# A hybrid decoder layer on one core: paired sums in the up projection, two interleaved blocks at the head of each down projection, six raw weight slots

## The chip, the cores and the metric

The kernel runs on one core of a Trainium2 chip. A core has a matrix engine (TensorE, PE in the profile, with its weight loads shown apart as PEld), a vector engine (VectorE, DVE), a scalar engine (ScalarE, ACT), GpSimd (POOL, idle here) and SyncE (SP), which issues every DMA of this kernel. Each engine works through its own list of instructions in order; semaphores make one wait for another. The metric is the device time of one launch in microseconds. The kernel before takes 2044.98 us as the median of three runs (2036.12 to 2045.6).

## What is computed

One decoder layer over 2064 positions (16 learned meta tokens and 2048 inputs), width 1024, in fp32:

```python
u = rmsnorm(h) ; p = u @ w_in                       # 1024 -> 1792
y = concat(pool(p_pool), conformer(p_bval, p_bgate), rglru(p_cgate, p_cx))
h = h + y @ w_out
u = rmsnorm(h)
h = h + square(relu(u @ w_up)) @ w_down             # 1024 -> 4096 -> 1024
out = rmsnorm(h)[:, 16:]
```

The three mixers are a windowed mean with a small group matmul, a gated depthwise convolution of 31 taps with a layer norm, and a gated linear recurrence with a convolution of 4 taps. Channels lie on the 128 partitions, positions along the free dimension.

## The kernel before, in words

**Precision.** fp32 operands are split in two: `hi` is the value rounded to the matmul's fp32r type (ScalarE, line 108) and `lo` the rest (VectorE, line 109). A product is three matmuls: hi·hi, hi·lo, lo·hi. Every weight is loaded, split and used again in each chunk of positions, so splitting weights is the largest piece of work on ScalarE and VectorE.

**Stages.** The positions form four chunks (c = 0 to 3) of 512. The list `items` is the order of the matrix work: W blocks (input projection), O blocks (output projection), and for each chunk four groups g of four U units followed by eight D blocks. In chunk 2 the eight O blocks of chunk 3 stand inside the last group of D blocks, after the first four of them. In chunk 3 the last group of D blocks is done in two halves of 256 positions.

**A U unit** (`up_unit`, from line 761) makes two of the 32 tiles of 128 up-projection rows for 512 positions with seven products in place of eight (a Strassen-Winograd scheme on 2 x 2 blocks). The position side has seven operands, named B11, B21, B22, T1, T2, T3, T4, each a pair of tiles that `gen_norm2` makes once for a chunk; the weight side has seven blocks of 128 x 512, four of them sums that `gen_sums` computes once, in chunk 0, and stores in DRAM (`sums`). A product is 12 matmuls of 256 columns into its own PSUM bank (`mm_block`, line 285). VectorE adds the products up (line 782, seven adds of 256 columns), ScalarE applies relu and two squares, and VectorE makes the low half of the square (line 799). The results are two tiles of `U`, the inputs of the D blocks.

**A D block** (`mm_tile`, line 275) is 24 matmuls of 512 columns: eight input tiles k = 0 to 7, three matmuls each. The last two, k = 6 and 7, come from the unit just before it. VectorE adds the result to `h` (line 803).

**Weights.** `Weights` runs ahead of the matrix work: `wr` holds raw weight halves of 128 x 512 (WR = 4 slots, filled by SyncE, line 139), `wh` holds split ones (WH = 5 slots). A U product takes one half, a W, O or D block two. A raw slot is free again when its split on VectorE is done; a split slot when the last matmul on it is done.

**What sets the order.** The code is written in the order of `items`; after each item `pump` emits as much of the side work (mixers, normalisation, sums) as a budget allows. A scheduler then places the instructions of each engine by priority, which is the order in the program unless the code raises it, as their inputs and buffers come free in its own estimate. After that the order on each engine is fixed. PSUM has eight banks: five for the main products (`pm`), three for side work (`pb`).

## Time and profile before

| | before |
|---|---|
| median of 3 runs | 2044.98 us (2036.12 to 2045.6) |
| profiled execution | 2042.66 us, of which span 2040.9 us |
| PE busy | 1950.3 us (96%) |
| DVE busy | 1587.7 us (78%) |
| ACT busy | 1119.3 us (55%) |
| mean granted clock of TensorE | 0.985 |

In a row of a view by groups stand the line, engine, operation, the names written and read (buffer numbers left out), shapes and count, then busy time, the mean of one in ns, and the idle time just before. In the view of waits a row reads "engine, what waits, what it waited for: us in total, times, longest". In a timeline row stand the start, the busy time, and in brackets the idle time before it and what ended that. In a row of windows stand the stretch, its length, the busy time and count on each engine, the granted clock, the DMA engines' share and the GB/s. A PE that is shown busy may still be slow, since its records overlap and their ends are modelled.

### The profile page before, as it was taken

The numbers are of one execution on the slowest core, as the hardware profiler recorded it, in microseconds if no ns is written. First come the engines' busy times: TensorE is split into PE (matmuls) and PEld (weight loads), VectorE is DVE, ScalarE is ACT, GpSimd is POOL, SyncE is SP. The second block draws the span as 40 slices with busy tenths as digits, with TensorE's granted clock in tenths as the row PEclk, the third lists the DMA queues.
The fourth block names the chain that finished last, engine by engine and source line by source line (L and its number), as shares of the span: only waits on it lengthen the run. The fifth ranks groups of instructions, "written<-read, shape, count | busy, mean of one in ns | idle before, by whom it ended". The sixth has DMA issues, their size and how long they took to land.

```text
span 2040.9 us, 31716 instructions
## 1 busy us (share of the span) xinstructions
PE 1950.3 (96%) x11220; PEld 1694.6 (83%) x11220; DVE 1587.7 (78%) x2749; ACT 1119.3 (55%) x1904; POOL 0.2 (0%) x4
## 2 busy tenths in 40 slices
PE   8999889899998989999999999999999999999997
PEld 7888688788876779788898778888979878889797
DVE  8987787898988899874776799986768487556477
ACT  6654453635685535664575553664657346345364
POOL 0000000000000000000000000000000000000000
PEclk9999999999998999999999999999999999999999
DMA  6324588737534435353444633444435425544354
GB/s 201 114 78 154 175 255 282 223 114 237 164 106 143 146 98 156 98 156 103 150 119 129 193 102 113 140 117 133 139 108 160 123 79 171 153 131 143 112 167 148
DMA packets 166958, 297.79 MB, mean 146 GB/s; under 512 B 18320, under 2 KB 24592, under 8 KB 166800
## 3 DMA queue, kind: packets, MB, share of 16 engines
q1 hardware_dynamic: 166800, 295.77, 47.7%
q8 instruction: 88, 1.44, 0.3%
q14 instruction: 70, 0.57, 0.1%
HBM read 268.43 MB, written 27.26 MB: 145 GB/s over the span
## 4 chain that ended last, share of the span: by engine, by line
PE 49%; DVE 17%; DMA 15%; ACT 13%; issue 6%; SPq 0%; DVEq 0%; ACTq 0%
PE pm L275 41%; PE pm L285 6%; DMA wr<-sums 6%; DVE wh L109 5%; ACT wh L108 4%; DMA wr<-d_w_down 2%; DMA xr<-d_xr 2%; ACT fr L798 2%; ACT U L797 2%; DVE H L109 1%; ACT fr L795 1%; DVE U L799 1%; DMA s<-d_w_up 1%; DVE fr L782 1%; DVE rs L320 1%
## 5 line engine op out<-in xcount | busy, mean ns | idle before, releaser
L275 PE MATMUL pm<-U,wh 128*128 128x512 f32 (+1 forms) x4272 | 987.7, 390 | 42.4 <-ACT U L797 17.4
L275 PEld LDWEIGHTS pm<-U,wh 128*128 128x128 f32 x4272 | 785.0, 191 | 229.6 <-ACT U L797 24.3
L108 ACT ACTIVATE wh<-wr 128x512 fp32r<-128x512 f32 x876 | 538.2, 627 | 739.5 <-PE pm L275 485.2
L109 DVE TENSOR_TENSOR wh<-wr,wh 128x512 fp32r<-128x512 f32 x876 | 595.3, 686 | 217.1 <-ACT wh L108 213.4
L285 PE MATMUL pm<-H,wh 128*128 128x256 f32 x5376 | 662.6, 284 | 22.0 <-DVE wh L109 9.4
L285 PEld LDWEIGHTS pm<-H,wh 128*128 128x128 f32 x5376 | 650.5, 190 | 35.2 <-DVE wh L109 14.6
L275 PE MATMUL pm<-H,wh 128*128 128x512 f32 (+1 forms) x1344 | 268.0, 357 | 9.3 <-ACT H L373 7.5
L275 PEld LDWEIGHTS pm<-H,wh 128*128 128x128 f32 x1344 | 224.4, 190 | 49.5 <-ACT H L373 7.5
L517 DVE SCALAR_TENSOR_TENSOR ca<-Pbv,vec,ca 128x512 f32<-128x512 f32 x180 | 127.4, 745 | 0.0
L803 DVE TENSOR_TENSOR h<-h,pm 128x512 f32<-128x512 f32 (+1 forms) x106 | 71.3, 673 | 66.7 <-PE pm L275 66.2
L782 DVE TENSOR_TENSOR fr<-pm,q 128x256 f32<-128x256 f32 x256 | 106.5, 417 | 2.3 <-PE pm L285 1.3
L799 DVE TENSOR_TENSOR U<-fr,U 128x512 fp32r<-128x512 f32 x128 | 86.0, 687 | 23.1 <-ACT fr L798 21.7
L782 DVE TENSOR_TENSOR q<-pm,q 128x256 f32<-128x256 f32 x192 | 79.9, 416 | 7.3 <-ACT q L785 3.2
L797 ACT ACTIVATE U<-fr 128x512 fp32r<-128x512 f32 x128 | 77.1, 619 | 0.8
L798 ACT ACTIVATE fr<-fr 128x512 f32<-128x512 f32 x128 | 76.8, 617 | 0.2
L329 DVE TENSOR_TENSOR ss<-ss,fr 128x512 f32<-128x512 f32 (+1 forms) x84 | 53.9, 642 | 13.1 <-ACT fr L328 12.8
L320 DVE RECIPROCAL rs<-rs 128x512 f32<-128x512 f32 (+2 forms) x17 | 53.9, 3168 | 10.9 <-ACT rs L318 10.9
L793 ACT ACTIVATE fr<-fr 128x512 f32<-128x512 f32 x64 | 39.9, 624 | 7.3 <-DVE fr L782 6.7
L517 DVE SCALAR_TENSOR_TENSOR ca<-h,vec,ca 128x512 f32<-128x512 f32 x60 | 42.4, 745 | 0.0
L795 ACT ACTIVATE fr<-fr 128x512 f32<-128x512 f32 x64 | 39.6, 619 | 0.5
L328 ACT ACTIVATE fr<-h 128x512 f32<-128x512 f32 (+1 forms) x45 | 27.4, 617 | 15.8 <-DVE h L697 8.8
L551 DVE SCALAR_TENSOR_TENSOR t<-Pcx,vec,t 128x512 f32<-128x512 f32 x36 | 26.8, 744 | 0.4 <-ACT t L549 0.3
(199 smaller groups left out, 1003.3 us busy)
## 6 DMA issues: line engine op xcount, KB each, us to landing
wr<-d_w_down SPq DMA_DIRECT2D x272, 256.0 KB, 3.0
wr<-sums SPq DMA_DIRECT2D x256, 256.0 KB, 3.3
wr<-d_w_up SPq DMA_DIRECT2D x192, 256.0 KB, 3.2
wr<-d_w_in SPq DMA_DIRECT2D x92, 256.0 KB, 3.2
xr<-d_xr SPq DMA_DIRECT2D x56, 256.0 KB, 3.2
t<-d_w_up SPq DMA_DIRECT2D x32, 256.0 KB, 4.1
wr<-wo_fold SPq DMA_DIRECT2D x32, 256.0 KB, 2.8
wr<-d_w_out SPq DMA_DIRECT2D x32, 256.0 KB, 2.7
```

Source lines behind the costliest of these rows:

```text
L108: A.activation(out=hi, in_=src, func=AF.Copy)
L109: V.tensor_tensor(out=lo, in0=src, in1=hi.bitcast(F32), op=ALU.subtract)
L275: T.matmul(ps[:, : s1 - s0], w[k // 4][:, a, (k % 4) * P : (k % 4 + 1) * P], rhs[k][:, b, s0:s1], start=(k == 0 and j == 0), stop=(k == KB ...
L285: T.matmul(ps, w[:, a, k * P : (k + 1) * P], op[k // 2][:, b, (k % 2) * 256 : (k % 2) * 256 + 256], start=(k == 0 and j == 0), stop=(k == ...
L320: V.reciprocal(rs[:, c0:c1], rs[:, c0:c1])
L517: V.scalar_tensor_tensor(out=a, in0=o.ub[i][:, k : k + NT], scalar=vc("cw", i * CONVK + k), in1=a, op0=ALU.mult, op1=ALU.add)
L782: V.tensor_tensor(out=out, in0=ps, in1=x, op=ALU.add)
L795: A.activation(out=ra, in_=ra, func=AF.Relu)
L797: A.activation(out=f[:, 0], in_=r, func=AF.Square)
L798: A.activation(out=r, in_=r, func=AF.Square)
L799: V.tensor_tensor(out=f[:, 1], in0=r, in1=f[:, 0].bitcast(F32), op=ALU.subtract)
L803: V.tensor_tensor(out=h, in0=h, in1=ps[:, : s1 - s0], op=ALU.add)
```

## The change

- **Unit.** The products come in the order B11, B21, T2, T1, T3, B22, T4, the weight blocks with them. B21 and T2 share a PSUM bank and are added to the first product by one add of 512 columns; T1 and T3 likewise; T4 is put beside T1, across two neighbouring banks, and one add of 512 columns finishes the second output tile. So a unit has three adds of 512 columns and one of 256 in place of seven of 256. The first output tile is finished before the last product. A unit takes three of the four `fr` work tiles instead of two.
- **PSUM.** Four banks for `pm`, one tile of two banks for `pw` (a single buffer), two banks for `pb`.
- **Down projection.** The first two D blocks of a group run together (`mm_pair`): six k of the first, six k of the second, then k = 6, 7 of the first and of the second. In chunk 3's last group this holds for the first half only.
- **Weights.** WR is 6, WH is 4, and a weight split gets a priority 200 instructions higher. The run-ahead of loads (WH + WR) goes from 9 to 10.
- **Normalisation.** `gen_norm2` makes its operands in an order that suits the new order of products; the amounts of work are the same.
- **Chunk 2.** The O blocks of chunk 3 come after two D blocks instead of four.

```diff
-WR = 4
-WH = 5
+WR = 6
+WH = 4
 LA_SPLIT = WH
+EARLY = 200
 LA_DMA = WH + WR
...
-    pm = es.enter_context(tc.tile_pool(name="pm", bufs=5, space=bass.MemoryType.PSUM))
-    pb = es.enter_context(tc.tile_pool(name="pb", bufs=3, space=bass.MemoryType.PSUM))
+    pm = es.enter_context(tc.tile_pool(name="pm", bufs=4, space=bass.MemoryType.PSUM))
+    pw = es.enter_context(tc.tile_pool(name="pw", bufs=1, space=bass.MemoryType.PSUM))
+    pb = es.enter_context(tc.tile_pool(name="pb", bufs=2, space=bass.MemoryType.PSUM))
...
                 t = t_("wh", (2, 512), WH, F32R)
-                split(t[:, 0], t[:, 1], self.raw.pop(self.ns))
+                with tc.high_priority(EARLY):
+                    split(t[:, 0], t[:, 1], self.raw.pop(self.ns))
...
+    def mm_pair(ws, rhs, sub):
+        s0, s1 = sub
+        pss = [ps_main() for _ in ws]
+        for ks in (range(KB - 2), range(KB - 2, KB)):
+            for w, ps in zip(ws, pss):
+                for k in ks:
+                    for j, (a, b) in enumerate(PRODS):
+                        T.matmul(
+                            ps[:, : s1 - s0], w[k // 4][:, a, (k % 4) * P : (k % 4 + 1) * P], rhs[k][:, b, s0:s1],
+                            start=(k == 0 and j == 0), stop=(k == KB - 1 and j == 2),
+                        )
+        return pss
...
     def up_unit(o, u, h0):
...
-        p1, q, q7, s5 = (q_tile() for _ in range(4))
-        A.activation(out=p1, in_=product(), func=AF.Copy)
-        add(q, product(), p1)
-        add(q7, product(), q)
-        ps = product()
-        add(rb[:, rgt], ps, q7)
-        add(s5, ps, q)
-        add(ra[:, lft], product(), p1)
-        add(rb[:, lft], product(), q7)
-        A.activation(out=rb, in_=rb, func=AF.Relu)
-        add(ra[:, rgt], product(), s5)
-        A.activation(out=ra, in_=ra, func=AF.Relu)
-        for f, r in ((fb, rb), (fa, ra)):
+        def add2(out, ps, x):
+            V.tensor_tensor(
+                out=out.rearrange("p (a c) -> p a c", a=2), in0=ps.rearrange("p (a c) -> p a c", a=2),
+                in1=x.unsqueeze(1).broadcast_to([P, 2, 256]), op=ALU.add,
+            )
+        def square(f, r):
+            A.activation(out=r, in_=r, func=AF.Relu)
             A.activation(out=f[:, 0], in_=r, func=AF.Square)
             A.activation(out=r, in_=r, func=AF.Square)
             V.tensor_tensor(out=f[:, 1], in0=r, in1=f[:, 0].bitcast(F32), op=ALU.subtract)
+        px, py, pz = ps_main(), ps_main(), pw.tile([P, 1024], F32, name=nm("pw"), tag="pw")
+        product(px[:, :256])
+        A.activation(out=p1, in_=px[:, :256], func=AF.Copy)
+        product(py[:, :256])
+        product(py[:, 256:])
+        add2(ra, py, p1)
+        q = ra[:, 256:]
+        product(pz[:, 512:768])
+        product(pz[:, 768:])
+        add2(t2, pz[:, 512:], q)
+        px = ps_main()
+        product(px[:, :256])
+        V.tensor_tensor(out=q, in0=px[:, :256], in1=t2[:, :256], op=ALU.add)
+        square(fa, ra)
+        product(pz[:, 256:512])
+        add2(rb, pz[:, 256:768], t2[:, 256:])
+        square(fb, rb)
...
-                items.extend(down[:4])
+                items.extend(down[:2])
                 items.extend(("O", 3, j, full) for j in range(KB))
-                items.extend(down[4:])
+                items.extend(down[2:])
...
+        if kind == "D" and j % KB == 0 and s0 == 0:
+            wts.ahead(wi)
+            ws = [[wts.hl.pop(wi + 2 * i + q) for q in range(2)] for i in range(2)]
+            pss = mm_pair(ws, o.f, (s0, s1))
+            evac_d(o, j // KB, 0, pss[0], s0, s1)
+            held_ps.append(pss[1])
+            pump(BUD_D)
+            continue
```

How it moves instructions is shown at three places. In the names, `wh` is a split weight half and `wr` the raw one, `pm` and `pw` are PSUM tiles, `U` an input tile of the D blocks, `fr` a work tile of a unit, `H` a split operand of the U units, `s` and `t` work tiles of the normalisation. The numbers are the program's own and differ between the kernels.

First, PE where the second group of chunk 2 goes from its last U unit to its D blocks. Before (the unit's last product, then a whole D block, then the next):

```order
L285 MATMUL pm_2545_14066<-H_2162_11922,wh_2531_13983 128x256 x6
L275 MATMUL pm_2548_14092<-U_2428_13481,wh_2534_14002 128x512 x3
L275 MATMUL pm_2548_14092<-U_2429_13482,wh_2534_14002 128x512 x3
L275 MATMUL pm_2548_14092<-U_2459_13637,wh_2534_14002 128x512 x3
L275 MATMUL pm_2548_14092<-U_2460_13638,wh_2534_14002 128x512 x3
L275 MATMUL pm_2548_14092<-U_2488_13787,wh_2537_14022 128x512 x3
L275 MATMUL pm_2548_14092<-U_2489_13788,wh_2537_14022 128x512 x3
L275 MATMUL pm_2548_14092<-U_2517_13937,wh_2537_14022 128x512 x3
L275 MATMUL pm_2548_14092<-U_2518_13938,wh_2537_14022 128x512 x3
L275 MATMUL pm_2554_14138<-U_2428_13481,wh_2540_14041 128x512 x3
```

Now (from k = 4 of the first block on):

```order
L292 MATMUL pm_2342_13768<-U_2292_13479,wh_2336_13719 128x512 x3
L292 MATMUL pm_2342_13768<-U_2293_13480,wh_2336_13719 128x512 x3
L292 MATMUL pm_2343_13769<-U_2242_13189,wh_2338_13741 128x512 x3
L292 MATMUL pm_2343_13769<-U_2243_13190,wh_2338_13741 128x512 x3
L292 MATMUL pm_2343_13769<-U_2268_13337,wh_2338_13741 128x512 x3
L292 MATMUL pm_2343_13769<-U_2269_13338,wh_2338_13741 128x512 x3
L292 MATMUL pm_2343_13769<-U_2292_13479,wh_2340_13763 128x512 x3
L292 MATMUL pm_2343_13769<-U_2293_13480,wh_2340_13763 128x512 x3
L292 MATMUL pm_2342_13768<-U_2316_13621,wh_2336_13719 128x512 x3
L292 MATMUL pm_2342_13768<-U_2317_13622,wh_2336_13719 128x512 x3
L292 MATMUL pm_2343_13769<-U_2316_13621,wh_2340_13763 128x512 x3
L292 MATMUL pm_2343_13769<-U_2317_13622,wh_2340_13763 128x512 x3
```

The last unit's two `U` tiles stood behind 18 matmuls of the D blocks and stand behind 36 now; four weight halves are in use at once where it was two.

Second, ACT at the same place. Before:

```order
L108 ACTIVATE wh_2537_14022<-wr_2526_13948 128x512
L108 ACTIVATE wh_2540_14041<-wr_2529_13967 128x512
L108 ACTIVATE wh_2543_14061<-wr_2532_13986 128x512
L793 ACTIVATE fr_2520_13940<-fr_2520_13940 128x512
L108 ACTIVATE wh_2546_14087<-wr_2535_14005 128x512
L797 ACTIVATE U_2518_13938<-fr_2520_13940 128x512
L795 ACTIVATE fr_2519_13939<-fr_2519_13939 128x512
L798 ACTIVATE fr_2520_13940<-fr_2520_13940 128x512
L797 ACTIVATE U_2517_13937<-fr_2519_13939 128x512
L798 ACTIVATE fr_2519_13939<-fr_2519_13939 128x512
```

Now:

```order
L110 ACTIVATE wh_2336_13719<-wr_2315_13602 128x512
L110 ACTIVATE wh_2338_13741<-wr_2326_13633 128x512
L801 ACTIVATE fr_2318_13623<-fr_2318_13623 128x512
L110 ACTIVATE wh_2340_13763<-wr_2328_13651 128x512
L802 ACTIVATE U_2316_13621<-fr_2318_13623 128x512
L801 ACTIVATE fr_2319_13624<-fr_2319_13624 128x512
L803 ACTIVATE fr_2318_13623<-fr_2318_13623 128x512
L802 ACTIVATE U_2317_13622<-fr_2319_13624 128x512
L110 ACTIVATE wh_2345_13834<-wr_2330_13668 128x512
L803 ACTIVATE fr_2319_13624<-fr_2319_13624 128x512
```

The relus and squares of the last unit still stand behind the splits of the next D weights; the first relu has moved up by one split, to the place before the last of the pair's four halves. A split for the third D block stands ahead of the last square in both.

Third, DVE in the input projection of chunk 2, where the operands of chunk 1's U units are made in between. Before, up to the next split of weights:

```order
L109 TENSOR_TENSOR H_1264_6999<-s_1294_7116,H_1264_6999 128x512
L109 TENSOR_TENSOR H_1265_7000<-t_1283_7057,H_1265_7000 128x512
L721 TENSOR_TENSOR t_1284_7061<-s_1293_7113,t_1284_7061 128x512
L714 SCALAR_TENSOR_TENSOR t_1301_7167<-h_1232_6856,vec_1_66,rs_1260_6993 128x256
L714 SCALAR_TENSOR_TENSOR t_1301_7167<-h_1240_6898,vec_1_66,rs_1260_6993 128x256
L109 TENSOR_TENSOR H_1266_7001<-t_1284_7061,H_1266_7001 128x512
L109 TENSOR_TENSOR H_1267_7002<-t_1275_7010,H_1267_7002 128x512
L109 TENSOR_TENSOR H_1268_7003<-t_1282_7052,H_1268_7003 128x512
L109 TENSOR_TENSOR H_1269_7004<-t_1301_7167,H_1269_7004 128x512
L721 TENSOR_TENSOR s_1292_7109<-t_1301_7167,s_1292_7109 128x512
L109 TENSOR_TENSOR wh_1302_7175<-wr_1287_7071,wh_1302_7175 128x512
L109 TENSOR_TENSOR wh_1303_7178<-wr_1288_7073,wh_1303_7178 128x512
```

Now:

```order
L111 TENSOR_TENSOR wh_1237_7176<-wr_1221_7052,wh_1237_7176 128x512
L738 TENSOR_TENSOR t_1201_6929<-t_1201_6929,t_1193_6882 128x512
L111 TENSOR_TENSOR H_1181_6870<-t_1193_6882,H_1181_6870 128x512
L111 TENSOR_TENSOR H_1186_6875<-t_1194_6887,H_1186_6875 128x512
L448 TENSOR_TENSOR Pcx_1236_7172<-pm_1235_7147,rs_1143_6688 128x512
L738 TENSOR_TENSOR t_1194_6887<-s_1212_6992,t_1194_6887 128x512
L111 TENSOR_TENSOR wh_1238_7179<-wr_1222_7054,wh_1238_7179 128x512
L738 TENSOR_TENSOR t_1202_6934<-t_1202_6934,t_1194_6887 128x512
L111 TENSOR_TENSOR H_1182_6871<-t_1194_6887,H_1182_6871 128x512
L111 TENSOR_TENSOR wh_1243_7215<-wr_1227_7104,wh_1243_7215 128x512
L111 TENSOR_TENSOR H_1183_6872<-t_1203_6939,H_1183_6872 128x512
L111 TENSOR_TENSOR H_1184_6873<-s_1210_6984,H_1184_6873 128x512
```

Ahead of the split of `wh_1302` stood ten and more instructions of normalisation in one piece; now two to five instructions stand between one weight split and the next.

More of the change, by code (lines that the diff above doesn't have):

```diff
@@ L730, in gen_norm2 @@
             put("B11", p, b11[p])
-            yield 1700
+            yield 1550
+        for p in range(2):
+            b21.append(norm(p, 1, 0))
+            put("B21", p, b21[p])
+            yield 1550
+        t1 = b11
         for p in range(2):
             b12.append(norm(p, 0, 1))
-            sub(b11[p], b12[p], b11[p])
-            t1.append(b11[p])
-            yield 1700
+            sub(t1[p], b12[p], b11[p])
+            yield 1550
         for p in range(2):
             b22.append(norm(p, 1, 1))
-            t2.append(t_(*(lambda g: (g[0], W0, g[1]))(free.pop()))[:, :NT])
-            sub(t2[p], b22[p], t1[p])
-            put("T2", p, t2[p])
-            yield 2400
-        for p in range(2):
             sub(b12[p], b22[p], b12[p])
-            put("T3", p, b12[p])
-            yield 1400
+            yield 1550
         free += [("s", SBF)] * SBF + [("t", TB)] * TB
+        t3 = b12
         for p in range(2):
             put("T1", p, t1[p])
-            yield 700
+            sub(t1[p], b22[p], t1[p])
+            put("T2", p, t1[p])
+            yield 2100
         for p in range(2):
-            b21 = norm(p, 1, 0)
-            put("B21", p, b21)
-            sub(t2[p], b21, t2[p])
-            put("T4", p, t2[p])
-            yield 3000
+            sub(b21[p], b21[p], t1[p])
+            put("T3", p, t3[p])
+            yield 1400
         for p in range(2):
             put("B22", p, b22[p])
-        yield 1400
+            put("T4", p, b21[p])
+            yield 1400
     def up_unit(o, u, h0):
@@ L764, in up_unit, with product @@
         o.f += [fa, fb]
-        ra, rb = t_("fr", W0, FR)[:, :NT], t_("fr", W0, FR)[:, :NT]
-        lft, rgt = slice(0, 256), slice(256, 512)
-        order = ("B11", "T2", "T3", "T1", "B21", "T4", "B22")
+        ra, rb, t2 = (t_("fr", W0, FR)[:, :NT] for _ in range(3))
+        p1 = t_("q", 256, 2)
+        order = ("B11", "B21", "T2", "T1", "T3", "B22", "T4")
         nxt = [h0]
-        def product():
+        def product(ps):
             h = nxt[0]
@@ L773, in product @@
             wts.ahead(h)
[L774 to L796 removed]
+            mm_block(ps, wts.hl.pop(h), o.u2[order[h - h0]])
+        def add2(out, ps, x):
[5 more added lines that the diff above has]
+            A.activation(out=r, in_=r, func=AF.Relu)
             A.activation(out=f[:, 0], in_=r, func=AF.Square)
@@ L924, in build @@
     mixes.append(Mix(ch[0]))
+    held_ps = []
     for n, it in enumerate(items):
@@ L937, in build @@
         wi = windex[n]
+        if kind == "D" and j % KB == 1 and held_ps:
+            evac_d(o, j // KB, j % KB, held_ps.pop(), s0, s1)
+            pump(BUD_D)
[6 more added lines that the diff above has]
+            held_ps.append(pss[1])
+            pump(BUD_D)
+            continue
         if kind != "U":
```

11 lines of the change are left out of this document (2 added, 9 removed).

## The prediction

> **What bounds the kernel now.** I read the page's first part, then PE's own waits, then stretches of the timeline where those waits fall.
>
> ```profile
> span 2040.9 us, 31716 instructions
> PE 1950.3 (96%) x11220; PEld 1694.6 (83%) x11220; DVE 1587.7 (78%) x2749; ACT 1119.3 (55%) x1904; POOL 0.2 (0%) x4
> 1852.20:1892.20 40.00, 40.00 (x338) 40.00 (x337) 30.72 (x59) 26.27 (x49) 0.00 (x0) 1.00 0.54 165
> 1414.60:1436.90 22.30, 22.30 (x97) 17.97 (x96) 8.21 (x12) 5.06 (x8) 0.00 (x0) 1.00 0.34 95
> core 0: 2040.9 us, clock 0.985
> ```
>
> PE sets the time. The two window rows are clean stretches: four U units run at 40.00/338 = 0.118 us a matmul (1.42 us a product, 9.9 us a unit), D blocks at 22.30/97 = 0.23 us. The change leaves the number of matmuls as it is, so it can only take away what PE loses to waits and to the clock. These are the waits of PE's weight loads, which meet a semaphore first:
>
> ```profile
> PEld pm L275 <- ACT U L797: 24.3, 16, 2.7
> PEld pm L275 <- DVE U L799: 17.6, 15, 1.7
> PEld pm L285 <- DVE wh L109: 14.6, 25, 1.6
> PEld pm L275 <- DVE wh L109: 11.7, 6, 5.6
> PEld pm L285 <- ACT wh L108: 10.0, 14, 1.9
> PEld pb L310 <- ACT hl L108: 9.5, 11, 4.1
> PEld pm L275 <- ACT wh L108: 7.8, 4, 2.5
> PEld pm L285 <- ACT H L108: 4.9, 9, 1.0
> PEld pm L285 <- DVE H L109: 3.7, 7, 0.8
> ```
>
> Four causes. The D blocks wait for the last unit's `U` tiles: 24.3 + 17.6 = 41.9 us, at 16 places, one for each group. Split weights are late: 14.6 + 11.7 + 10.0 + 7.8 = 44.1 us. The start of a chunk's U units: 9.5 us for the column sum and 4.9 + 3.7 = 8.6 us for operands. All nine rows are 104.1 us, 5% of the span. Half clock comes on top:
>
> ```profile
> 484.85 4.36 PE L275 MATMUL pm<-U,wh 128*128 128x512 f32 x18
> 491.51 0.50 PE L275 MATMUL pm<-U,wh 128*128 128x512 f32 x1 [2.30 <-ACT U L797]
> 492.90 3.41 PE L275 MATMUL pm<-U,wh 128*128 128x512 f32 x8 [0.89 <-DVE U L799]
> ```
>
> After this wait eight matmuls took 3.41 us, 0.43 each and not 0.23, so the stall cost another 1.6 us. A mean clock of 0.985 is 2 x 0.015 x 2040.9 = 61 us at half clock, worth at most 30 us, part of it spent waiting.
>
> **1. The paired D blocks.** The rows just shown are one such place: 18 matmuls, then a wait for k = 6, and at 492.90 the last tile is there, 8.05 us after the group's start. Another, and chunk 3's last group:
>
> ```profile
> 300.98 4.36 PE L275 MATMUL pm<-U,wh 128*128 128x512 f32 x18
> 309.19 3.06 PE L275 MATMUL pm<-U,wh 128*128 128x512 f32 x12 [0.51 <-DVE U L799]
> 1978.76 2.80 PE L275 MATMUL pm<-U,wh 128*128 128x256 f32 x22
> 1983.55 4.79 PE L275 MATMUL pm<-U,wh 128*128 128x256 f32 x26 [1.99 <-ACT U L797]
> ```
>
> There the last tile comes 8.21 us in. With the pair, k = 6 is first wanted after 36 x 0.23 = 8.3 us and k = 7 0.7 us later. So even tiles as late as these are just in time, and they should be earlier: the first tile is finished before the last product, and its lateness came in part from ScalarE standing at a split whose load had not landed:
>
> ```profile
> 1395.45 0.63 ACT L108 ACTIVATE wh<-wr 128x512 fp32r<-128x512 f32 x1 [1.40 <-DMA wr<-d_w_down]
> 1397.20 0.61 ACT L793 ACTIVATE fr<-fr 128x512 f32<-128x512 f32 x1
> ```
>
> In chunk 3's halves the cover is 36 x 0.118 = 4.2 us against 4.79: 0.5 us stays. What is late next: the pair holds four split halves, which is all four slots, so the third block's halves can be split only when the first two come free, 12 and 30 matmuls in (2.8 and 6.9 us), and are wanted at 48 matmuls (11.1 us). A split costs 1.3 us (rows below), so 2.9 us are spare. DVE stands at the second of these splits, and behind it the mixers of that stretch; nobody on PE waits for them there. Bounds: 20 us, if ordering keeps half the lateness, to 42. I take 39, nearest to the two places measured.
>
> **2. Weights: slots and place in the queue.**
>
> ```profile
> L109 DVE TENSOR_TENSOR wh<-wr,wh 128x512 fp32r<-128x512 f32 x876 | 595.3, 686 | 217.1 <-ACT wh L108 213.4
> L108 ACT ACTIVATE wh<-wr 128x512 fp32r<-128x512 f32 x876 | 538.2, 627 | 739.5 <-PE pm L275 485.2
> wr<-sums SPq DMA_DIRECT2D x256, 256.0 KB, 3.3
> ACT wh L108 <- DMA wr<-sums: 88.0, 71, 3.9
> ```
>
> A raw slot is taken for a load (3.3 us) and a split (0.63 + 0.69), 4.6 us in all. In U units one is wanted every 1.42 us: four slots give 5.7 us, 1.1 spare; six give 8.5, 3.9 spare. SyncE issues the next load only when VectorE's split is done, so each delay of VectorE goes into this loop. Against it stands the split slot: its cycle is a product (1.42) and a split (1.32); five slots leave 4.4 us spare, four 2.9.
>
> The place in the queue shows where the input projection stops:
>
> ```profile
> 708.62 0.68 DVE L109 TENSOR_TENSOR wh<-wr,wh 128x512 fp32r<-128x512 f32 x1
> 719.22 1.29 DVE L109 TENSOR_TENSOR wh<-wr,wh 128x512 fp32r<-128x512 f32 x2
> 719.95 6.26 PE L275 MATMUL pm<-U,wh 128*128 128x512 f32 x15 [5.12 <-DVE wh L109]
> ```
>
> For 10.6 us VectorE worked on normalisation and split no weight; PE stood 5.12 us, and its next 15 matmuls took 6.26 us where 3.5 is the rate. In the new order no such piece stands there. What is pushed back is normalisation and mixers, due at the next U or O blocks. I take two thirds of the 19.5 us of L275 (13) and, since the shorter `wh` works against the longer `wr`, under half of the 24.6 us of L285 (11): 24 together. Bounds: a loss of 20 (rival B in part) to a gain of 44.
>
> **3. Start of a chunk's units.** Two operands instead of one need no difference, so two products can go ahead early; chunk 3's normalisation gets 11 us more cover from the moved O blocks. The mixers that O needs are done in time: their last split is
>
> ```profile
> 1581.72 1.89 DVE L109 TENSOR_TENSOR H<-Pz,H 128x512 fp32r<-128x512 f32 x3
> 1574.00:1666.20 92.20, 90.36 (x389) 72.17 (x388) 59.31 (x94) 38.60 (x65) 0.00 (x0) 1.00 0.38 112
> ```
>
> and the O blocks would start 11 us after 1574. Their 16 weight loads and eight `xr` loads go past four others on SyncE's queue, in a stretch where the DMA engines are 38% busy. In chunk 0 VectorE makes operands, sums and splits and is 88% busy (row under rival A), so little is won there. Of 18.1 us I take 7 (bounds 3 to 15).
>
> **4. Adds.**
>
> ```profile
> L782 DVE TENSOR_TENSOR fr<-pm,q 128x256 f32<-128x256 f32 x256 | 106.5, 417 | 2.3 <-PE pm L285 1.3
> L782 DVE TENSOR_TENSOR q<-pm,q 128x256 f32<-128x256 f32 x192 | 79.9, 416 | 7.3 <-ACT q L785 3.2
> L803 DVE TENSOR_TENSOR h<-h,pm 128x512 f32<-128x512 f32 (+1 forms) x106 | 71.3, 673 | 66.7 <-PE pm L275 66.2
> ```
>
> The view of groups has 448 adds, 186 us. Now 192 of 512 columns at the 0.673 us of L803 and 64 at 0.417: 156 us. That is 30 us of VectorE, half a microsecond a unit, and it lies beside PE: counted as nothing by itself. Without that cover, where VectorE is the bound (rival A), it is worth at most the 16 units of chunk 0, 8 us.
>
> **5. What it costs.** One bank less for main products and for side work, one `pw` tile, three `fr` tiles of four. No row shows a wait for a PSUM bank, so the bounds are 0 and, for one late bank a U group at the longest wait of PE for an evacuated operand above (1.0 us), 16 us. I take 4, nearer zero. Fewer stalls give back some half clock: 4 us (bounds 0 to 15).
>
> [...]
>
> **Sum.** 39 + 24 + 7 + 4 - 4 = 70 us. The profiled execution took 2042.7 us (1.8 more than its span): 1973. The median of the runs is 2.3 us above it, so 1975.
>
> **Rivals.** A: *VectorE is the bound.*
>
> ```profile
> 245.40:774.40 529.00, 494.57 (x2678) 420.03 (x2677) 468.13 (x807) 288.08 (x491) 0.00 (x0) 0.97 0.56 174
> ```
>
> Here it is busy 468 of 529 us, 88%; PE is idle 34. If late weights there are a matter of VectorE's amount and not of order, term 2 and its clock go: 1975 + 24 + 4 = 2003. Against it: work in one piece runs tighter than 88%, and 30 us go. B, the other side: *four split slots starve the units.* A split has 2.9 us for its turn on two in-order engines; a unit's three ScalarE steps in a row (0.61 each, the relu's row above) and one add of 0.67 on VectorE use most of it. If one product a unit comes 1.6 us late (the longest wait of L285 on DVE above), 64 units lose 102 us: 1975 + 102 = 2077, slower. It decides from 70/64 = 1.1 us a unit. Against it: splits are ranked first. C: *the pair waits for its weights instead*, four halves being wanted where it was two: half of term 1 goes, 1995. D: *shared banks hold PE.* The fourth product of a unit needs the `pw` tile that the unit before frees with its last add: 3 x 1.42 = 4.3 us for one split and one add, 1.4 us. It bites only where VectorE is over 2.9 us late; 1 us in each of 64 units gives 2039, no change. [...] That the pair does nothing is excluded by PE's new order.
>
> **Chances.** Forecast 0.62 (its own range 1948 to 1993, the upper end with 18 us less of term 2), A 0.18, C 0.06, B 0.10, D 0.04. From no change this kernel's measurement tells about 0.5%, 10 us. Faster: forecast, A, C and a little of D, 0.87; the same, the rest of D and a mild B, 0.04; slower 0.09. The range goes from 1948 (2045 - 42 - 44 - 7 - 8 + 4: terms 1 and 2 at their upper bounds and half of the clock's) to 2014, which is A with term 5 near its own bound (11 us more).
>
> **What would show it.** PE's waits for `U` under 8 us and no wait at matmul 18 of a group; no piece of 10 us without a weight split on VectorE in the input projections; ScalarE's waits for `wr` well under the 88 us for `sums`; VectorE's busy time down by about 30 us. Wrong it is if PE's waits for `wh` in U units grow past 24.6 us (B), or PE waits for an add before a unit's fourth product (D).

## The result and the profile after

The changed kernel takes 1994.55 us in the median (1989.49 to 1996.8, four runs) beside 2045.29 us for the kernel before (2036.12 to 2052.92, four runs): a ratio of 0.975, 95% interval 0.9706 to 0.9795, so some 50 us faster. The forecast was 1975 us with a range of 1948 to 2014: the time lies inside the range, and the gain is 50 us where 70 were forecast. It lies 1.5 us above 1993, where the forecast's own part of the range ended; the part from there to 2014 had been opened for rival A.

The first part of the page of the changed kernel, and in a second fence its span with the mean granted clock:

```profile
span 1987.7 us, 31314 instructions
PE 1927.7 (97%) x11220; PEld 1685.3 (85%) x11220; DVE 1580.9 (80%) x2557; ACT 1127.3 (57%) x1907; POOL 0.2 (0%) x4
```

```profile
core 0: 1987.7 us, clock 0.992
```

VectorE has 192 instructions less and is busy only 7 us less (1587.7 before). The clock is 0.992, before 0.985. Now the waits of PE's weight loads, the view that carried the prediction (engine, what waits, what it waited for: us in total, times, longest). Line 278 is the block of W, O and D (275 before), 302 a U product (285 before), 327 the column sum (310 before):

```profile
PEld pb L327 <- ACT hl L110: 13.5, 11, 6.5
...
PEld pw L302 <- issue: 7.2, 7, 3.3
PEld pw L302 <- DVE H L111: 5.1, 2, 4.6
...
PEld pm L302 <- DVE wh L111: 4.4, 7, 1.2
PEld pw L302 <- DVE fr L795: 3.7, 9, 0.6
PEld pm L278 <- DVE wh L111: 3.6, 5, 1.3
...
PEld pw L302 <- ACT wh L110: 2.6, 2, 1.8
PEld pw L302 <- DVE wh L111: 2.6, 3, 1.1
...
PEld pm L302 <- ACT wh L110: 1.8, 4, 0.6
...
PEld pm L278 <- ACT wh L110: 1.5, 1, 1.5
```

No row names `U` any more: the 41.9 us of D blocks waiting for the last unit's tiles are gone. The six rows of `wh` add up to 16.5 us, where the four of before had 44.1. The column sum waits longer, 13.5 us for 9.5. And there is a wait that the kernel before does not have: products into `pw` wait for an add (`fr`, line 795). The row of `issue` is mostly the same stop seen at the weight loads: its three longest pieces (3.34, 2.21 and 0.74 us) stand in front of the same products. It is clearer in the waits of the matmuls themselves and, at one place, in the timelines of PE and VectorE (start, busy time, instruction, and in brackets the idle time before it and what ended it):

```profile
PE pw L302 <- DVE fr L795: 9.2, 10, 3.2
```

```profile
457.97 1.65 PE L302 MATMUL pw<-H,wh 128*128 128x256 f32 x12 [3.16 <-DVE fr L795]
...
456.53 0.69 DVE L197 TENSOR_TENSOR t<-s,t 128x512 f32<-128x512 f32 x1 [1.98 <-DMA s<-d_w_up]
457.14 0.68 DVE L795 TENSOR_TENSOR fr<-pw,fr 128x512 f32<-128x512 f32 x1
```

The 12 matmuls at 457.97 are a unit's seventh product. It goes into the first bank of the two-bank tile `pw`. The fourth and fifth product lie in the second bank, and the add at 457.14 reads them: it touches no column that the seventh product writes, and yet the product starts only when that add is done. Between the fifth and the seventh product PE has one product to do, 1.42 us, so an add that is later than that stops PE. Here it stood on VectorE behind a difference of raw weights whose load was late (1.98 us). All ten waits of that row stand in front of a seventh product, none in front of a fourth.

What PE loses can be put down to stages if each stretch is measured from its first matmul to the next stretch's first, and its matmuls are taken off at the clean rates (0.118 us for 256 columns, 0.121 for 264, 0.232 for 512). This is worked out from the traces, one profiled execution each and good to some 3 us a cell, for four kernels that the next section needs:

| us lost by PE | before | changed | changed, seventh product in a tile of its own | the same, with six banks for all |
|---|---|---|---|---|
| first group of U units | 15.9 | 11.2 | 11.3 | 11.3 |
| the other 15 groups of U units | 28.4 | 26.9 | 12.5 | 11.8 |
| all other stages | 94.5 | 47.4 | 47.7 | 32.2 |
| sum | 138.8 | 85.5 | 71.5 | 55.3 |

From the first column to the second, nearly all the gain lies outside the U units (47 of 53 us). In the U units the better supply of weights should have shown, and 1.5 us in 15 groups is what is left of it.

### The profile page after: what moved, and what is told of

It reads as the page before. It is cut to its first block, busy times and chain, and to the rows that moved or that the text cites. A ratio compares the mean times of both kernels' runs of the same rounds, so it can differ in the third digit from the quotient of the medians.

```text
span 1987.7 us, 31314 instructions
## 1 busy us (share of the span) xinstructions
PE 1927.7 (97%) x11220; PEld 1685.3 (85%) x11220; DVE 1580.9 (80%) x2557; ACT 1127.3 (57%) x1907; POOL 0.2 (0%) x4
## 4 chain that ended last, share of the span: by engine, by line
PE 73%; DVE 13%; DMA 5%; issue 4%; ACT 4%; SPq 0%; DVEq 0%; ACTq 0%
PE pm L278 41%; PE pm L302 13%; PE pw L302 11%; PE pm L292 7%; DVE wh L111 3%; DMA xr<-d_xr 2%; DMA s<-d_w_up 1%; DVE ca L534 1%; DVE fr L795 1%; ACT wh L110 1%; DVE t L568 1%; PE pb L311 1%; DVE H L111 0%; DVE h L828 0%; DVE U L804 0%
## 5 line engine op out<-in xcount | busy, mean ns | idle before, releaser
L110 ACT ACTIVATE wh<-wr 128x512 fp32r<-128x512 f32 x876 | 546.0, 627 | 669.7 <-PE pm L278 411.5
L278 PE MATMUL pm<-U,wh 128*128 128x512 f32 (+1 forms) x3504 | 790.2, 384 | 1.4 <-DVE wh L111 1.3
L278 PEld LDWEIGHTS pm<-U,wh 128*128 128x128 f32 x3504 | 634.7, 188 | 143.3 <-DVE wh L111 3.1
L302 PE MATMUL pm<-H,wh 128*128 128x256 f32 x3072 | 392.7, 283 | 4.7 <-DVE wh L111 2.9
L302 PEld LDWEIGHTS pm<-H,wh 128*128 128x128 f32 x3072 | 378.4, 189 | 9.2 <-DVE wh L111 4.4
L302 PE MATMUL pw<-H,wh 128*128 128x256 f32 x2304 | 301.4, 284 | 16.5 <-DVE fr L795 9.2
L302 PEld LDWEIGHTS pw<-H,wh 128*128 128x128 f32 x2304 | 284.9, 190 | 22.3 <-issue 7.2
L278 PE MATMUL pm<-H,wh 128*128 128x512 f32 (+1 forms) x1344 | 272.9, 361 | 13.5 <-ACT H L390 7.3
L278 PEld LDWEIGHTS pm<-H,wh 128*128 128x128 f32 x1344 | 227.7, 193 | 55.7 <-ACT H L390 7.3
L292 PE MATMUL pm<-U,wh 128*128 128x512 f32 (+1 forms) x768 | 176.5, 388 | 0.0
L292 PEld LDWEIGHTS pm<-U,wh 128*128 128x128 f32 x768 | 140.0, 188 | 30.9
L828 DVE TENSOR_TENSOR h<-h,pm 128x512 f32<-128x512 f32 (+1 forms) x106 | 71.2, 674 | 49.7 <-PE pm L278 35.9
L795 DVE TENSOR_TENSOR fr<-pw,fr 128x512 f32<-128x512 f32 x128 | 87.8, 686 | 5.5 <-PE pw L302 3.1
L795 DVE TENSOR_TENSOR fr<-pm,q 128x512 f32<-128x512 f32 x64 | 43.7, 683 | 2.8 <-PE pm L302 2.4
```

The source lines that it names most:

```text
L110: A.activation(out=hi, in_=src, func=AF.Copy)
L278: T.matmul(ps[:, : s1 - s0], w[k // 4][:, a, (k % 4) * P : (k % 4 + 1) * P], rhs[k][:, b, s0:s1], start=(k == 0 and j == 0), stop=(k == KB ...
L292: T.matmul(ps[:, : s1 - s0], w[k // 4][:, a, (k % 4) * P : (k % 4 + 1) * P], rhs[k][:, b, s0:s1], start=(k == 0 and j == 0), stop=(k == KB ...
L302: T.matmul(ps, w[:, a, k * P : (k + 1) * P], op[k // 2][:, b, (k % 2) * 256 : (k % 2) * 256 + 256], start=(k == 0 and j == 0), stop=(k == ...
L795: V.tensor_tensor(out=out.rearrange("p (a c) -> p a c", a=2), in0=ps.rearrange("p (a c) -> p a c", a=2), in1=x.unsqueeze(1).broadcast_to([ ...
L828: V.tensor_tensor(out=h, in0=h, in1=ps[:, : s1 - s0], op=ALU.add)
```

## The experiments

Each ratio is to the kernel before, run on the same chip beside it. Unless said otherwise an edit is made to the changed kernel. Beside the experiments the kernel before took 2041.45 to 2045.29 us, and the interval of the changed kernel's own ratio is some 9 us to either side; a difference to the changed kernel that is smaller than that is not shown by the medians.

### 1. Without the interleaved pair

```diff
-        if kind == "D" and j % KB == 1 and held_ps:
-            ...
-        if kind == "D" and j % KB == 0 and s0 == 0:
-            ...
-            pss = mm_pair(ws, o.f, (s0, s1))
-            ...
```

> The changed kernel with its first two D blocks one after the other again, all else kept. Theory (the pair is what hides the last unit's tiles): PE's waits for U come back at the 16 groups, some 30 to 42 us of them, and with a little half clock the time is 2025 to 2040. Rival (the deeper weight queue already brings the tiles early, the pair is worth little): waits for U stay under 12 us and the time is 1995 to 2008.

Measured: 1995.78 us, 0.9773 (0.9753 to 0.9792), no difference to the changed kernel that these intervals show (1 us by the medians, 7 by the profiled spans), as the rival expected. The waits for `U` are back, but small; and here is a D block's start in this kernel, on PE and VectorE:

```profile
PEld pm L278 <- DVE U L804: 5.4, 9, 2.7
```

```profile
1286.35 11.36 PE L278 MATMUL pm<-U,wh 128*128 128x512 f32 x48
...
1288.86 0.68 DVE L804 TENSOR_TENSOR U<-fr,U 128x512 fp32r<-128x512 f32 x1
...
1290.13 0.68 DVE L804 TENSOR_TENSOR U<-fr,U 128x512 fp32r<-128x512 f32 x1
```

The two tiles are done 3.2 and 4.5 us after the D block's start. Without the pair they are wanted 18 and 21 matmuls in, at 4.2 and 4.9 us: just in time. In the kernel before, at the same group:

```profile
1303.18 4.35 PE L275 MATMUL pm<-U,wh 128*128 128x512 f32 x18
1309.22 0.49 PE L275 MATMUL pm<-U,wh 128*128 128x512 f32 x1 [1.68 <-ACT U L797]
...
1303.09 1.28 ACT L108 ACTIVATE wh<-wr 128x512 fp32r<-128x512 f32 x2 [2.07 <-DMA wr<-d_w_down]
...
1306.45 0.63 ACT L108 ACTIVATE wh<-wr 128x512 fp32r<-128x512 f32 x1 [1.00 <-DMA wr<-d_w_down]
...
1309.05 1.50 DVE L799 TENSOR_TENSOR U<-fr,U 128x512 fp32r<-128x512 f32 x2
```

There the last tile is done 7.4 us in, after ScalarE stood 2.07 + 1.00 us for raw weights. So the tiles come 2.9 us earlier without the pair, about as much as ScalarE stood for loads. The new unit also squares its first tile before the last product, where the old one did all squares after it; how much is the unit's doing and how much the loads' was not run apart.

### 2. The pair alone, in the kernel before

The mirror image: the pair's code from the diff is put into the kernel before, and nothing else.

> The kernel before with nothing but the paired D blocks. Theory (the pair's gain stands by itself): waits for U fall from 41.9 us to under 5, time 1998 to 2010. Rival (four halves wanted at once from four raw slots: the pair waits for weights instead): waits for wh in the D blocks grow by 15 us or more, time 2018 to 2035.

Measured: 2015.43 us, 0.9868 (0.985 to 0.9886), 28 us faster than the kernel before, between what the theory and the rival allowed. Its waits for weights:

```profile
PEld pm L299 <- DVE wh L109: 18.3, 32, 1.6
PEld pm L275 <- DVE wh L109: 12.0, 8, 5.5
PEld pm L275 <- ACT wh L108: 10.3, 6, 2.8
PEld pm L299 <- ACT wh L108: 9.1, 13, 2.4
```

Of the 41.9 us of waits for `U` 1.6 us at two places are left: the pair does what it says. But late weights rise from 44.1 to 49.7 us, presumably because PE, no longer stopped, reaches the next weights earlier. In this kernel the pair is worth 28 us, in the changed one nothing that can be told from noise; with experiment 1 that is a shared wait. The pair covers it and the earlier tiles remove it, and the second of two cures earns nothing.

### 3. Old weight slots, and no rank

```diff
-WR = 6
-WH = 4
+WR = 4
+WH = 5
-                with tc.high_priority(EARLY):
-                    split(t[:, 0], t[:, 1], self.raw.pop(self.ns))
+                split(t[:, 0], t[:, 1], self.raw.pop(self.ns))
```

> The changed kernel with four raw slots, five split slots and no raised rank for splits, all else kept. Theory (slots and rank removed the late weights): PE's waits for wh go from 13 back towards 44 us, time 2015 to 2030. Rival (the late weights were a consequence of the stalls at the D blocks, and of VectorE's amount of work): waits for wh stay under 22 us, time under 2006.

And with the new slots kept, only the rank taken away:

> The changed kernel with six and four slots but no raised rank for splits. Theory (the rank cures the input projections, the slots the U units): pieces of ten and more VectorE instructions without a weight split come back and cost 10 to 20 us in the L278 blocks, time 2003 to 2015; PE's waits for column sums fall below the 13.5 us that they have now. Rival (the slots alone do it): time within 6 us of 1994.5.

Measured: 2014.24 us, 0.987 (0.984 to 0.9899) for both; 2005.16 us, 0.9817 (0.9795 to 0.9839) without the rank. So weights are worth 20 us in the changed kernel, 11 of it the rank and 9 the slots by the medians; how the 20 divide is not sure, since each part is near the interval of the changed kernel. The time with both taken back is 0.8 us below what the theory allowed, and late weights come back to 30.2 us, not to 44. ScalarE's wait for the raw sums, in the changed kernel, without the rank, and with the old slots; then the largest wait of PE's loads without the rank, and PE's waits for the add with the old slots:

```profile
ACT wh L110 <- DMA wr<-sums: 0.7, 1, 0.7
```

```profile
ACT wh L110 <- DMA wr<-sums: 4.6, 4, 2.0
...
PEld pm L277 <- DVE wh L111: 16.9, 5, 7.4
```

```profile
ACT wh L110 <- DMA wr<-sums: 66.8, 56, 5.6
...
PE pw L301 <- DVE fr L794: 27.8, 33, 4.5
```

The slots take ScalarE's stalls away (88.0 us in the kernel before), the rank takes the long waits of single blocks (16.9 us at five places, against 3.6). The last row shows two parts of the change touching each other: with four raw slots the seventh product's wait is three times the 9.2 us, where without the rank alone it is 3.6 us. It is the slots, then; that an engine which stands at a load also brings the add late is the likely way, not shown step by step.

### 4. The seventh product in a bank of its own

The two-bank tile goes; there are six banks for all products. The last paired add becomes two adds of 256 columns.

```diff
-    pm = es.enter_context(tc.tile_pool(name="pm", bufs=4, ...))
-    pw = es.enter_context(tc.tile_pool(name="pw", bufs=1, ...))
+    pm = es.enter_context(tc.tile_pool(name="pm", bufs=6, ...))
-        px, py, pz = ps_main(), ps_main(), pw.tile([P, 1024], F32, ...)
+        px, py, pz = ps_main(), ps_main(), ps_main()
...
+        add2(t2, pz, q)
+        V.tensor_tensor(out=rb[:, 256:], in0=pz[:, :256], in1=t2[:, 256:], op=ALU.add)
...
-        product(pz[:, 256:512])
-        add2(rb, pz[:, 256:768], t2[:, 256:])
+        px = ps_main()
+        product(px[:, :256])
+        V.tensor_tensor(out=rb[:, :256], in0=px[:, :256], in1=t2[:, 256:], op=ALU.add)
```

> The changed kernel in which the seventh product has a PSUM bank of its own and the last paired add is two adds of 256 columns, one of them before the seventh product (six banks of one kind, no two-bank tile). One more VectorE instruction a unit, 0.15 us. Theory (the seventh product waits for the add of T1 and T3, because both lie in the two-bank tile): PE's waits for that add, 9.2 us, go to under 1, and with their half clock the time falls by 8 to 15 us, to 1980 to 1987. Rival (VectorE is late in chunk 0 whatever waits for it; the stall moves to the next product or to the weights): chunk 0's first three groups lose as much as now, time 1990 to 1998.

Measured: 1962.28 us, 0.9604 (0.9582 to 0.9625): 32 us faster than the changed kernel, outside what both the theory and the rival allowed and far more than the waits for the add. Two things were changed at once, the shared tile and the number of banks that every stage may use; sections 5 and 6 take them apart.

### 5. The same with four banks

```diff
-    pm = es.enter_context(tc.tile_pool(name="pm", bufs=6, ...))
+    pm = es.enter_context(tc.tile_pool(name="pm", bufs=4, ...))
```

> The seventh product in a bank of its own, as in the run that took 1962 us, but only four banks for all products instead of six (the two that the shared tile held stay empty). Theory, the tile: the gain of 32 us came from taking the seventh product off the tile that the add of the fifth and sixth reads, so four banks are enough: within 6 us of 1962. Rival, the banks: the gain came largely from two more banks for the products of every other stage; then the 8.5 us that the stretch with the gate's products of chunk 2 gained, and the part of the units' losses that comes from banks, come back: 1975 to 1992. If slower than 1995, a unit needs more than four banks to run ahead of its adds.

Measured: 1988.52 us, 0.9732 (0.971 to 0.9755). The time is outside the bounds of the tile's theory and inside those of the banks'; it is not told apart from the changed kernel. But a unit holds four banks here, which is all there are, so the units have less than in the changed kernel too. By stage PE loses 13.1, 15.9 and 56.5 us (the three rows of the table): against the changed kernel the units gain 9 us and the other stages lose 9. What was missing is a kernel with the changed kernel's own deal of banks.

### 6. Only the shared tile undone

```diff
-    pw = es.enter_context(tc.tile_pool(name="pw", bufs=1, ...))
+    pw = es.enter_context(tc.tile_pool(name="pw", bufs=2, ...))
-        px, py, pz = ps_main(), ps_main(), pw.tile([P, 1024], F32, ...)
+        px, py, pz = ps_main(), ps_main(), pw.tile([P, 512], F32, ...)
...
+        V.tensor_tensor(out=rb[:, 256:], in0=pz[:, :256], in1=t2[:, 256:], op=ALU.add)
...
-        product(pz[:, 256:512])
-        add2(rb, pz[:, 256:768], t2[:, 256:])
+        px = pw.tile([P, 512], F32, ...)
+        product(px[:, :256])
+        V.tensor_tensor(out=rb[:, :256], in0=px[:, :256], in1=t2[:, 256:], op=ALU.add)
```

As in section 4 the last paired add becomes two adds of 256 columns, one of them ahead of the seventh product.

> Only the shared tile is undone: the same eight banks are dealt out as in the changed kernel (four for all products, two for the units of the up projection alone, two for sums), but the units' two are now two tiles of one bank, the fourth and fifth product in the one and the seventh in the other, so that the seventh no longer waits for the add of the fourth and fifth. Theory, the tile: the other stages need no more banks and most of the 32 us come: 1962 to 1974. Rival, banks for all: what gave the 32 us was that every stage may run six products ahead; dealt out as before, only the 12.9 us of waits of the seventh product can go, and as with four banks alone (1988.5) some of that comes back as waits for late weights: 1980 to 1992.

Measured: 1974.06 us, 0.9653 (0.9635 to 0.9671), just past the upper edge of what the tile's theory allowed and below the banks'. So of the 32 us some 20 are the shared tile's (1994.55 - 1974.06; by the profiled spans 14) and some 12 the banks' (by the spans 15). That the split add is not what did it is seen in section 8, where the paired adds stay and the wait goes too. The table says where. With the tile undone the 15 later groups of U units lose 12.5 us and not 26.9, and the other stages the same 47. With six banks for all the units stay and the other stages fall to 32.2. Two stretches show it, chunk 0's second group of U units and the stretch of D blocks, output and input projection at the end of that chunk (columns: the stretch, its length, then busy time and count of PE, its weight loads, VectorE, ScalarE and GpSimd, the granted clock, the DMA engines' share, GB/s), in the changed kernel, in this one, and with six banks:

```profile
341.50:390.00 48.50, 43.20 (x338) 41.94 (x337) 47.09 (x84) 31.23 (x55) 0.00 (x0) 0.96 0.82 268
568.20:761.20 193.00, 180.69 (x751) 142.03 (x750) 168.38 (x269) 108.13 (x171) 0.00 (x0) 0.97 0.38 116
```

```profile
345.40:385.40 40.00, 40.00 (x338) 39.99 (x337) 39.61 (x71) 28.10 (x51) 0.00 (x0) 1.00 0.91 300
563.90:756.20 192.30, 180.49 (x750) 142.34 (x749) 168.98 (x271) 108.98 (x172) 0.00 (x0) 0.97 0.38 117
```

```profile
339.80:379.80 40.00, 40.00 (x338) 40.00 (x337) 39.93 (x72) 28.08 (x51) 0.00 (x0) 1.00 0.94 311
557.90:742.50 184.60, 177.54 (x751) 140.90 (x750) 163.22 (x264) 111.16 (x174) 0.00 (x0) 0.99 0.40 122
```

These units go from 48.50 to 40.00 us by the tile alone, which is the clean rate; the other stretch stays at 193 until it has six banks. Not every group gains: chunk 0's third loses some 3 us more than in the changed kernel, at late weights (3.32 us at one place). Waits of a block for the evacuation of an earlier one stand only where four banks are: in the changed kernel (1.3 and 1.1 us) and in this one (the rows shown), but in no row of the six-bank kernel:

```profile
PE pm L278 <- DVE h L448: 1.6, 1, 1.6
PE pm L278 <- DVE h L714: 1.1, 1, 1.1
...
PE pb L327 <- ACT hl L110: 8.0, 4, 5.0
```

The first two are 2.7 us of the 15. The largest piece of the rest, some 6 us, is a column sum (the last row, 5.0 us at one place), next.

### 7. The column sum behind late loads of x

In the changed kernel, 673.40 us after the start, the column sum of chunk 2's x stands on PE before its data are there. The first two rows of the fence are of ScalarE, which squares x as it comes:

```profile
665.70 0.63 ACT L345 ACTIVATE fr<-xr 128x512 f32<-128x512 f32 x1 [2.16 <-DMA xr<-d_xr]
...
671.33 0.63 ACT L345 ACTIVATE fr<-xr 128x512 f32<-128x512 f32 x1 [2.21 <-DMA xr<-d_xr]
...
673.40 0.79 PE L327 MATMUL pb<-hl,ones 128*128 128x512 f32 x1 [6.03 <-ACT hl L110]
674.13 0.79 PE L328 MATMUL pb<-hl,ones 128*128 128x512 f32 x1
674.73 7.34 PE L278 MATMUL pm<-H,wh 128*128 128x512 f32 x24
```

PE is stopped for 6.03 us, and the 24 matmuls behind take 7.34 us instead of 24 x 0.232 = 5.57. From the start of the stop to the end of these matmuls are 14.70 us, and the 26 matmuls in them take 6.03 at the clean rate: 8.7 us are lost. One edit gives x a third buffer:

```diff
-        raw = t_("xr", NT, 2)
+        raw = t_("xr", NT, 3)
```

(at all four places that use `xr`).

> The changed kernel with three buffers instead of two for the raw rows of x. Theory (the column sums before an input projection stand on PE ahead of their data, which comes late because a load of x waits on SyncE's queue for one of two buffers): the wait of 6.03 us at the column sum before chunk 2's input projection, and the 1.86 us at chunk 3's, shrink to under 2 us together, time 1983 to 1990. Rival (those loads wait behind the weight loads on SyncE's queue, not for a buffer): the waits stay, time 1992 to 1997.

The same on top of experiment 4:

> The seventh product in a bank of its own and three buffers for the loads of x and of the raw conv rows instead of two. Theory: the column sums still wait 8.0 + 4.7 us in the run of 1962 us, and the first unit of chunk 0 loses 10.7; the third buffer takes most of the first away and some of the second: 1948 to 1957. Rival: with the shared tile gone these waits are short and TensorE catches up nothing: 1959 to 1965. What no theory expects: slower than 1965, which would mean that the earlier loads push the weights back.

Measured: 1978.41 us, 0.9684 (0.9661 to 0.9708) in the changed kernel, 16 us faster than it by the medians and 7 by the profiled spans, below what its theory allowed; 1960.68 us, 0.9601 (0.9581 to 0.9622) on top of experiment 4, where it changes nothing, as the rival expected. In the changed kernel with the third buffer the longest wait at a column sum is 1.9 us:

```profile
PE pb L327 <- ACT hl L110: 5.2, 3, 1.9
```

In experiment 4's kernel the same column sum was placed later in PE's order and waits 1.33 us:

```profile
662.80 0.50 PE L326 MATMUL pb<-hl,ones 128*128 128x512 f32 x1 [1.33 <-ACT hl L109]
```

So the 8.7 us lost at this place in the changed kernel are cured by a buffer or by banks: again two cures for one wait. What the median gained beyond them was not traced.

### 8. The seventh product made earlier, and less work for VectorE

In the first edit the operand T4 is made and its product issued before T1 and T3, so that it does not stand behind their add.

```diff
...
-        order = ("B11", "B21", "T2", "T1", "T3", "B22", "T4")
+        order = ("B11", "B21", "T2", "T4", "T1", "T3", "B22")
...
```

The operands, the weight blocks and the adds follow this order; the paired adds and the two-bank tile stay.

> The changed kernel with product T4 put ahead of T1 and T3, so that all three of the two-bank tile's products are written before its first add; the paired adds stay, the last product is B22 with an add of 256. Theory (the wait is one product writing a tile that an add still reads): waits of the two-bank tile's products for adds under 2 us, time 1980 to 1988. Rival (VectorE's lateness moves the stall): 1990 to 1998. T4's operand is wanted earlier at a chunk's start: there the first units may lose 2 to 4 us more.

The second leaves out most taps of chunk 1's convolution.

```diff
-        for k in range(1, CONVK):
+        for k in range(1, 3 if o.c == 1 else CONVK):
```

> The changed kernel with two of the 30 added taps of chunk 1's depthwise convolution instead of all (56 VectorE instructions of 0.745 us left out, 42 us between the start of chunk 0's U units and chunk 1's output projection; this leaves out part of the convolution for chunk 1). Theory A (VectorE's amount of work is the bound of that stretch): the stretch's loss of 50 us falls by 25 or more, time 1960 to 1970. Rival (single waits in order, for sums' loads, operands and column sums, not the amount): the loss falls by less than 12, time 1983 to 1995.

Measured: 1980.89 us, 0.9699 (0.9671 to 0.9726), with no wait for the add left among its rows; and 1982.9 us, 0.9702 (0.9678 to 0.9726). The first agrees with section 6 from another side: 14 us for getting that product away from the add. It pays for it at chunk 3's first group of U units, where PE loses some 6 us more than in the changed kernel; 2 to 4 had been expected. The second takes 38.5 us of VectorE's work away (1580.9 to 1542.4 us busy) and gains 11.7, less than a third, so the amount of VectorE's work is not the bound; section 6 gains more with no work removed.

### 9. The pair once more, without the shared tile

The edit of section 1 on top of that of section 4.

> The seventh product in a bank of its own, and the down projection's first two sums one after the other as in the kernel before. Theory: inside the changed kernel the interleaving hides no wait, since the tiles of U already come in time; without it 1959 to 1966 us. Rival: the interleaving was worth nothing only because the shared tile set the pace; without the shared tile its absence shows, up to the 28 us it was worth alone in the kernel before: 1975 to 1990.

Measured: 1961.33 us, 0.9603 (0.9583 to 0.9624), against 1962.28 with the pair. In its trace the D blocks wait 9.8 us for tiles, and the time is the same:

```profile
PEld pm L277 <- DVE U L803: 9.8, 16, 1.6
```

PE's other waits are shorter by as much: all rows of the matmuls' own waits add up to 30.1 us here and to 30.2 with the pair. So the shared tile did not hide the pair's worth: where tiles are early, the pair is worth nothing that is seen. The kernels of sections 4 and 9 and the second of section 7 are the fastest seen, 1961 to 1962 us, 4% below the kernel before, and do not differ from each other.

## Where the prediction was right and where not

**Bound and sign: right.** PE sets the time, the number of its matmuls is unchanged, and the gain is stall time and a little clock.

**Step 1 (the pair, 39 us): the mechanism right, its worth in this kernel wrong.** Every wait for `U` went, as forecast. But the price was taken from the kernel before as though the rest of the change did not touch that wait. Alone the pair brings 28 us, not 39, in part since 5.6 us come back as late weights; together with the rest it brings nothing measurable (sections 1 and 9). The prediction had even noted that the tiles' lateness came in part from ScalarE standing at loads, and did not carry this over to term 1. Rival C, that the pair waits for its weights, holds for the pair alone, at 5.6 us where it was priced at 20.

**Step 2 (weights, 24 us): right in size.** Taking slots and rank back costs 20 us. Late weights fell from 44.1 to 16.5 us: by 14.4 in the blocks and 13.2 in the units, where 13 and 11 had been taken. Rival B did not come: waits for weights in U units are 11.4 us (4.4 + 2.6 + 2.6 + 1.8), not over 24.6. What the steps 1 and 2 share, the early tiles, cannot be booked to one of them; the sum of the two, 63 us, stands against 47 us gained outside the U units and 1.5 in their later groups.

**Step 3 (start of a chunk's units, 7 us gained): about right at its place, wrong in what it counted there.** At the starts themselves the rows fell: the column sum ahead of chunk 0's units waits 0.25 us where it waited 4.10 (the two rows, before and now), and the rows for the operands `H` add up to 7.0 us against 8.6, all of it now in chunk 0. But the step had put all 9.5 us of column sums down to the units' starts, and some belong to the sums of x ahead of the input projections. Those grew, at the weight loads from 0.61 to 6.46 us in chunk 2 and from 0.75 to 2.29 in chunk 3, so that the row as a whole went from 9.5 to 13.5 us. That loss was in no term; the column sum's place in PE's order and the two buffers of x decided it (section 7).

```profile
229.71 0.19 PEld L310 LDWEIGHTS pb<-hl,ones 128*128 128x128 f32 x1 [4.10 <-ACT hl L108]
```

```profile
228.75 0.19 PEld L327 LDWEIGHTS pb<-hl,ones 128*128 128x128 f32 x1 [0.25 <-ACT hl L110]
```

**Step 4 (adds, counted as nothing): right for the end, wrong for VectorE.** The expected 30 us less came out as 7. The groups of adds (count, then busy time, mean of one in ns, and idle time before) are what was reckoned, and the second fence has two neighbours of VectorE's timeline:

```profile
L795 DVE TENSOR_TENSOR fr<-pw,fr 128x512 f32<-128x512 f32 x128 | 87.8, 686 | 5.5 <-PE pw L302 3.1
...
L795 DVE TENSOR_TENSOR fr<-pm,q 128x512 f32<-128x512 f32 x64 | 43.7, 683 | 2.8 <-PE pm L302 2.4
...
L820 DVE TENSOR_TENSOR fr<-pm,fr 128x256 f32<-128x256 f32 x64 | 26.8, 418 | 2.0 <-PE pm L302 0.9
```

```profile
453.26 0.68 DVE L795 TENSOR_TENSOR fr<-pm,q 128x512 f32<-128x512 f32 x1
453.87 0.68 DVE L111 TENSOR_TENSOR wh<-wr,wh 128x512 fp32r<-128x512 f32 x1
```

They add up to 158 us against 186. But the two neighbours show an instruction starting 0.61 us after one of 0.68: neighbours overlap by some 0.07 us, so a view of durations counts that part twice, and 192 fewer instructions save 0.07 x 192 = 13 us less than their durations say (an estimate). The whole view bears it out: the durations of all groups of VectorE add up to 1728.0 us before and 1706.7 now, while its busy time is 1587.7 and 1580.9, so the time counted twice fell by 14.5 us. The adds' durations fell by 28 us, those of the other instructions rose by 7, and 14.5 had been counted twice: that leaves the 7.

**Step 5 (fewer banks and one tile, 4 us, at most 16): the term that failed.** The shared tile costs 20 us by the medians (14 by the spans), and four banks in place of six for the other stages 12 more; what four cost against the five of the kernel before was not run. The bound had been set from the kernel before, where no row shows a wait for a bank; but there five banks were free to all. Rival D had the right object and the wrong place and price: not the next unit's fourth product, with 4.3 us to spare, but the same unit's seventh, with 1.42 us, because the tile is waited for as a whole although the two products touch different banks of it. That the seventh product writes one bank and the add reads the other was not enough here: the product at 457.97 stood 3.16 us until the add was done, and with a tile for each bank the time goes from 1994.55 to 1974.06 us (section 6).

**The sum.** 70 us were forecast and 50 came. Without the shared tile (experiment 6) it would have been 2044.6 - 1974.1 = 70.5, the forecast almost to the microsecond. That the match is so close is luck. The tile's 20 us are shown, but the other terms were not each worth what they were booked at: steps 1 and 2 overlap, the banks cost 12 us more, and the 8.7 us at the column sum of x were in no term. The clock's term had 4 us, at most 15; by the prediction's own way of reckoning, time at half clock (0.50 granted, as from 494.00 to 496.00 us in the kernel before) went from 61 to 2 x 0.008 x 1987.7 = 32 us, so at most 15 us came from there, and how much of that is already counted in the waits is open. The time lies in the range only by the part opened for rival A, whose reason did not hold.

**Rival A** (VectorE is the bound in chunk 0, 2003 us) came nearer the time by number (8.5 us off against 19.6), but by luck and not by its reason: in the six-bank kernel the same stretch runs in 499.5 us where the changed kernel takes 518.1, with all of VectorE's work, and the second edit of section 8 gained under a third of the work it took away.

## What to carry to other kernels

When two parts of a change cure the same wait, price them together: the wait can be gained once, and whether each part is needed shows only when it is taken out of the finished kernel. Before several accumulations share one tile, find the product that writes it again soonest and compare the time until then (here 1.42 us) with the latest the reading add can be, since the wait may be for the tile and not for the bank. And a wait that no row shows is no bound for a kernel that has less of that resource.

## What the runs showed that was not expected

The two-bank tile makes PE wait for a read of the other bank (457.97, 3.16 us), and one tile for each bank removes it. Banks act on waits that name no bank: six for all cut the other stages' loss from 47.7 to 32.2 us, in good part because PE's order came out differently, with the column sum at another place in it (5.0 us of wait in section 6, 1.33 with six banks). The 6.03 us stall cost 8.7 us in all; the next 24 matmuls took 7.34 us instead of 5.57, at a granted clock of 0.77 (0.50 from 673.40 to 677.40, 1.00 from 678.40 on). In the kernel before the two stops of 2.30 and 0.89 us at 491.51 and 492.90 were followed by 0.57 over 3.45 us; in the changed kernel 1.00 stood behind the 3.16 us at 457.97. How long a stop brings the clock down was not shown. Left open: the first group of U units loses some 9 to 16 us in every kernel run here, in the changed kernel 5.1 of its 11.2 in waits for the operand `H` of the first products (4.35 and 0.72 us), and nothing tried was aimed at it.
